# The lower part of every third weight chunk in the first layer's mixers made by an adding DMA instead of VectorE, with rings one deeper

## The chip, the cores and the metric

The kernel runs on one core of one Trainium2 chip. The time is that of the device, in microseconds (us), as the median of several runs. In the profile PE is TensorE's matmul, PEld its weight load, DVE is VectorE, ACT ScalarE, POOL GpSimd, and SP the engine that issues the loads.

## The reference

Two layers of a block on x of 256 × 1024 numbers in f32. Each layer normalizes x, multiplies it by one wide matrix, and feeds the pieces to three mixers: attention with low-rank projections (8 heads), gated linear attention (GLA, 4 heads) and a diagonal state-space scan (S5). Their outputs, each through a projection of its own, are merged by sigmoid gates and projected once more; a feed-forward part with a squared relu follows.

```python
for l in range(2):
    h = rms_norm(x, norm1_g[l])
    z = h @ w_in[l]
    (cq, ckv, kpe, gq, gk, gv, glr, gr, su, gates) = split_in(z)
    o_a = mla_mixer(cq, ckv, kpe, ...)        # attention
    o_b = gla_mixer(gq, gk, gv, glr, gr, ...) # gated linear attention
    o_c = s5_mixer(su, ...)                   # scan over a complex diagonal state
    g = sigmoid(gates + gate_b[l]).reshape(B, L, 3, D)
    merged = g[:, :, 0] * (o_a @ w_br_mla[l]) + g[:, :, 1] * (o_b @ w_br_gla[l]) + g[:, :, 2] * (o_c @ w_br_s5[l])
    x = x + merged @ w_out[l]
    h2 = rms_norm(x, norm2_g[l])
    x = x + square(relu(h2 @ w_ff1[l])) @ w_ff2[l]
```

## The kernel before

All weights of both layers stand in one tensor in memory, `wst`, as chunks of 128 × 1024 f32 numbers (512 KB; three chunks per layer are 128 × 768). The kernel goes through them once, in one stream of 276 chunks, 138 per layer: 73 for the mixers, gates and projections, then 64 for the feed-forward part. A chunk's place in the stream is called k here. The order is written out by hand in the table STEPS: each word is a step (su, qk, gv, gr for projections of x; s0 to s3 and y for the scan; h and p for the scores and the values of a head; g for gates; b for the branch projections; o for the output), a number behind "~" shifts the priority of its instructions. A scheduler turns the priorities into one fixed order of instructions on each engine, when the kernel is built.

A matmul is done in three passes on numbers cut into an upper and a lower part (`mm3`, L184 to L186): upper by upper, upper by lower, lower by upper. So each weight chunk passes through these stations:

- `fetch` (L144) issues the load of the chunk from SP's queue into a ring of three `raw` tiles.
- `prep` (L153) makes the two parts: ScalarE casts raw into hi (L164), rounded to the upper part, and VectorE subtracts, lo = raw − hi (L165).
- PE reads hi and lo. They live in two rings of NHI = 4 tiles each, and when the stream stands at chunk k, the chunks up to k + AHEAD, with AHEAD = 3, are prepared. A cast waits until PE is done with the chunk that held its place in the ring.

Beside the chunks, ScalarE and VectorE do the work of the mixers. Early in the first layer the function around L406 to L418 makes the S5 matrices: VectorE computes complex products in z, ScalarE spreads them into bbar (L418), PE transposes bbar into Btp (L453). At the same time the GLA gate runs through ScalarE: ab (L947, L948), the scan cs on VectorE (L951), the exponentials ep, en, dec (L956 to L960), with a load of the activation table ahead of some. In the softmax, ScalarE computes ppt (L875, exponentials, and L879, their scaling), PE transposes it into PTp. POOL only clears tiles and copies the scan's coefficients into R (L606).

Of the kernel before, what the change touches and what calls it, by code (L numbers as in the profile page):

```python
# [8 lines left out]
F32 = mybir.dt.float32  # L9
# [4 lines left out]
AF = mybir.ActivationFunctionType  # L14
ALU = mybir.AluOpType
# [40 lines left out]
CIDX = {c: i for i, c in enumerate(CHUNKS)}  # L56
# [30 lines left out]
class Kern:  # L87
# [67 lines left out]
    def prep(self, k):  # L155
        nc = self.nc
        l, c = self.stream[k]
        n = CCOLS.get(c[0], CW)
        self.prefetch(k + 1)
        raw = self.raws[k]  # L160
        hi = self.ring.tile([128, CW], F32R, tag="hi", name="hi", bufs=self.NHI)
        lo = self.ring.tile([128, CW], F32R, tag="lo", name="lo", bufs=self.NHI)
        for h in self.halves(k, n):
            nc.scalar.copy(hi[:, h], raw[:, h])  # L164
            nc.vector.tensor_tensor(out=lo[:, h], in0=raw[:, h], in1=hi[:, h].bitcast(F32), op=ALU.subtract)  # L165
        return hi, lo

    def w(self, l, c):
        assert self.stream[self.pos] == (l, c), (self.stream[self.pos], l, c)
        self.prepare(self.pos + 1 + self.AHEAD)  # L170
        t = self.prepped[self.pos]
        self.prepped[self.pos] = None
        self.pos += 1
        return t
# [989 lines left out]
    NPS = {"g": 2, "ps": 2, "acc": 4}  # L1164
    NSM = {"gv": 2, "v": 2, "gt": 2, "tmp": 3}
    NRAW = 3
    NHI = 4
    AHEAD = 3


    STEPS = [
# [194 lines left out]
    Kern(ctx, tc, aps).run()  # L1366


# [13 lines left out]
```

## Time and profile before

| what | us |
| --- | --- |
| median of 3 runs | 882.55 |
| lowest and highest | 882.38, 883.68 |
| profiled execution | 882.19 |
| its span, first to last instruction | 880.4 |
| PE busy | 861.7 |
| VectorE busy | 694.5 |
| ScalarE busy | 522.0 |
| POOL busy | 25.4 |

The mean granted clock of TensorE is 0.998 of full speed. Busy times are those of the profiled execution; matmuls overlap, so a group's sum of durations is larger than the time that it takes from the span. The stretches of the first layer are, roughly: start to 20 us; projections, GLA and the S5 matrices to 105; scan, attention and the first gates to 200; gates, branch and output projections to 265; the feed-forward part to 450. The second layer follows in the same manner.

### The profile page before, as it was taken

To read this page: it belongs to the slowest core of one execution; us is meant where nothing else is said; L and a number is where in the kernel's file an instruction comes from. 1 tells how busy PE (TensorE), PEld (TensorE's weight loads), DVE (VectorE), ACT (ScalarE), POOL (GpSimd) and SP (SyncE) were. 2 spreads that over 40 slices of the span, in tenths; PEclk is the share of its full clock that TensorE was granted. 3 is DMA by queue.
4 is the path that set the end of the run, shared out by engine and by line. 5 is a ranking of instruction groups with operands and counts; after the bars stand their busy time and mean duration, and the time that the engine had idled before them with its cause. 6 is when DMAs were issued, how large, how long until landed. Compare 5 with 4: busy or idle time off the path is not lost.

```text
span 880.4 us, 15290 instructions
## 1 busy us (share of the span) xinstructions
PE 861.7 (98%) x5900; PEld 771.2 (88%) x5900; DVE 694.5 (79%) x1339; ACT 522.0 (59%) x818; POOL 25.4 (3%) x35
## 2 busy tenths in 40 slices
PE   7999999999999999999999999999999999999998
PEld 6889988899988888888888989898999888888886
DVE  7999999987767986996677887899877776666664
ACT  6877887654456575664457647874554654444442
POOL 2000001010000000000000000002000000000000
PEclk9999999999999999999999999999999999999999
DMA  7534434245564565566545544244555555555562
GB/s 265 188 118 143 154 121 145 72 153 177 189 210 153 186 212 168 182 189 203 190 146 168 191 146 150 97 144 135 178 166 170 191 181 192 189 189 188 192 190 92
DMA packets 42264, 147.73 MB, mean 168 GB/s; under 512 B 4688, under 2 KB 5328, under 8 KB 42192
## 3 DMA queue, kind: packets, MB, share of 16 engines
q1 hardware_dynamic: 42192, 146.76, 51.6%
q8 instruction: 46, 0.75, 0.3%
q14 instruction: 26, 0.21, 0.1%
HBM read 145.70 MB, written 1.05 MB: 167 GB/s over the span
## 4 chain that ended last, share of the span: by engine, by line
PE 84%; DVE 10%; ACT 3%; issue 2%; DMA 1%; SPq 0%; DVEq 0%
PE fp L206 14%; PE fp L210 7%; PE fo L184 7%; PE fo L186 7%; PE fo L185 7%; PE gp L184 3%; DVE lo L165 3%; PE gp L185 3%; PE gp L186 3%; PE brp L184 2%; PE brp L186 2%; PE brp L185 2%; PE wo L186 2%; PE wo L184 2%; PE wo L185 2%
## 5 line engine op out<-in xcount | busy, mean ns | idle before, releaser
L165 DVE TENSOR_TENSOR lo<-raw,hi 128x1024 fp32r<-128x1024 f32 (+2 forms) x276 | 333.0, 1208 | 118.6 <-ACT hi L164 117.5
L164 ACT CAST hi<-raw 128x1024 fp32r<-128x1024 f32 (+2 forms) x276 | 286.1, 1038 | 234.0 <-PE fo L186 52.9
L206 PE MATMUL fp<-h,hi 128*128 128x512 f32 x512 | 180.5, 398 | 0.0
L210 PE MATMUL fp<-h,lo 128*128 128x256 f32 x512 | 133.5, 281 | 0.0
L184 PE MATMUL gp<-h,hi 128*128 128x256 f32 x384 | 109.9, 292 | 1.0 <-ACT ppt L875 0.8
L206 PEld LDWEIGHTS fp<-h,hi 128*128 128x128 f32 x512 | 93.9, 188 | 18.1
L186 PE MATMUL gp<-h,lo 128*128 128x256 f32 x384 | 107.8, 286 | 0.0
L185 PE MATMUL gp<-h,hi 128*128 128x256 f32 x384 | 107.4, 285 | 0.0
L210 PEld LDWEIGHTS fp<-h,lo 128*128 128x128 f32 x512 | 96.8, 189 | 5.5
L184 PE MATMUL fo<-hi,r 128*128 128x512 f32 x256 | 100.1, 391 | 0.0
L186 PE MATMUL fo<-hi,r 128*128 128x512 f32 x256 | 99.7, 390 | 0.0
L185 PE MATMUL fo<-lo,r 128*128 128x512 f32 x256 | 99.7, 389 | 0.0
L184 PEld LDWEIGHTS gp<-h,hi 128*128 128x128 f32 x384 | 72.7, 192 | 2.9 <-ACT ppt L875 1.0
L185 PEld LDWEIGHTS gp<-h,hi 128*128 128x128 f32 x384 | 72.6, 191 | 1.0 <-issue 0.5
L186 PEld LDWEIGHTS gp<-h,lo 128*128 128x128 f32 x384 | 72.7, 192 | 0.1
L185 PEld LDWEIGHTS fo<-lo,r 128*128 128x128 f32 x256 | 48.1, 188 | 10.1
L186 PEld LDWEIGHTS fo<-hi,r 128*128 128x128 f32 x256 | 48.1, 188 | 10.2
L184 PEld LDWEIGHTS fo<-hi,r 128*128 128x128 f32 x256 | 48.1, 188 | 8.8
L1133 ACT COPY fa<-fp 128x256 f32<-128x256 f32 x64 | 23.4, 367 | 29.3 <-PE fp L206 29.1
L1134 DVE TENSOR_TENSOR fa<-fa,fp 128x256 f32<-128x256 f32 x64 | 26.2, 416 | 13.7 <-ACT fa L1133 13.7
L1071 ACT ACTIVATE gt<-gt,hgateb 128x256 f32<-128x256 f32 x48 | 21.9, 501 | 9.0 <-DVE gt L1068 8.8
L256 ACT CAST r<-fa 128x512 fp32r<-128x512 f32 x32 | 19.9, 622 | 9.7 <-DVE fa L1135 9.5
(396 smaller groups left out, 1768.0 us busy)
## 6 DMA issues: line engine op xcount, KB each, us to landing
raw<-wst SPq DMA_DIRECT2D x266, 512.0 KB, 3.6
raw<-wst SPq DMA_DIRECT2D x6, 384.0 KB, 3.0
x<-xin SPq DMA_DIRECT2D x4, 256.0 KB, 4.6
raw<-wst SPq DMA_DIRECT2D x4, 256.0 KB, 5.6
bc_raw<-bcin SPq DMA_DIRECT2D x4, 256.0 KB, 3.8
out_dram<-x SPq DMA_DIRECT2D x4, 256.0 KB, 2.0
par<-parin SPq DMA_DIRECT2D x2, 205.0 KB, 5.8
masks<-consts SPq DMA_DIRECT2D x1, 128.0 KB, 3.8
```

The costliest lines, as they stand in the source:

```text
L164: nc.scalar.copy(hi[:, h], raw[:, h])
L165: nc.vector.tensor_tensor(out=lo[:, h], in0=raw[:, h], in1=hi[:, h].bitcast(F32), op=ALU.subtract)
L184: mm(out, lhsT=lt[0], rhs=rt[0], start=start, stop=False)
L185: mm(out, lhsT=lt[0], rhs=rt[1], start=False, stop=False)
L186: mm(out, lhsT=lt[1], rhs=rt[0], start=False, stop=stop)
L206: up = lambda: mm(flat, lhsT=w[0][:, c], rhs=self.h2[:, k].rearrange("p i t -> p (i t)"), start=k == 0, stop=k == KD - 1)
L210: mm(out[:, 0, :], lhsT=w[1][:, c], rhs=self.h[k][0], start=False, stop=False)
L256: nc.scalar.copy(hi, src)
L1071: nc.scalar.activation(g[:, m, :], g[:, m, :], AF.Tanh, scale=0.5, bias=self.small[l]["gateb"][:, c:c + 1])
L1133: nc.scalar.copy(a[:, m], p[:, 1, :])
L1134: self.mark = v.tensor_tensor(out=a[:, m], in0=a[:, m], in1=p[:, 0, :], op=ALU.add)
```

## The change

For 23 chunks, every third from k = 9 to k = 75, the lower part is no longer made by VectorE. ScalarE casts raw into hi as before, then writes −hi into lo, and POOL issues a DMA that adds the chunk from memory onto lo. The load of raw stays, so these chunks are transferred twice. One of the 23 is 128 × 768, the rest are 128 × 1024. Both rings have five tiles, and chunks are prepared four ahead. The last hunk sets the memory for descriptors of such transfers. Lines of the changed kernel below `prep` stand eight higher.

```diff
         hi = self.ring.tile([128, CW], F32R, tag="hi", name="hi", bufs=self.NHI)
         lo = self.ring.tile([128, CW], F32R, tag="lo", name="lo", bufs=self.NHI)
+        if self.by_dma(k):
+            nc.scalar.copy(hi[:, 0:n], raw[:, 0:n])
+            nc.scalar.activation(lo[:, 0:n], hi[:, 0:n].bitcast(F32), AF.Copy, scale=-1.0)
+            nc.gpsimd.dma_start(lo[:, 0:n], self.wst[l, CIDX[c], :, 0:n], accum_op=ALU.add)
+            return hi, lo
         for h in self.halves(k, n):
             nc.scalar.copy(hi[:, h], raw[:, h])
             nc.vector.tensor_tensor(out=lo[:, h], in0=raw[:, h], in1=hi[:, h].bitcast(F32), op=ALU.subtract)
         return hi, lo
+
+    def by_dma(self, k):
+        return 8 < k < 76 and k % 3 == 0
...
-    NHI = 4
-    AHEAD = 3
+    NHI = 5
+    AHEAD = 4
...
+BACC_KW = {"dynamic_dma_scratch_size": 4096}
...
-    nc = bacc.Bacc("TRN2", target_bir_lowering=False, num_devices=1)
+    nc = bacc.Bacc("TRN2", target_bir_lowering=False, num_devices=1, **BACC_KW)
```

The instructions move on ScalarE and POOL. First ScalarE ahead of the S5 matrices bbar and the Btp transposes, between the gate's logarithm (ab) and its exponentials (ep, en, dec); z with a number is VectorE's product, cmat the other S5 matrix. Before:

```order
L948 ACT_TABLE_LOAD
L948 ACTIVATE ab<-ab,half 128x512
L164 CAST hi<-raw 128x1024
L956 ACT_TABLE_LOAD
L956 ACTIVATE ep<-cs 128x512
L957 ACTIVATE en<-cs 128x512
L960 ACTIVATE dec<-cs 128x8
L164 CAST hi<-raw 128x1024
L418 ACTIVATE bbar<-z_476 64x16x16 x4
L164 CAST hi<-raw 128x1024
L418 ACTIVATE bbar<-z_477 64x16x16 x4
L418 ACTIVATE cmat<-z_478 64x16x16 x2
```

And after the change:

```order
L956 ACT_TABLE_LOAD
L956 ACTIVATE ab<-ab,half 128x512
L164 CAST hi<-raw 128x1024
L165 ACTIVATE lo<-hi 128x1024
L169 CAST hi<-raw 128x1024
L426 ACTIVATE bbar<-z_482 64x16x16 x4
L169 CAST hi<-raw 128x1024
L426 ACTIVATE bbar<-z_483 64x16x16 x4
L426 ACTIVATE cmat<-z_484 64x16x16 x2
L964 ACT_TABLE_LOAD
L964 ACTIVATE ep<-cs 128x512
```

The table load and the exponentials moved from ahead of bbar to behind it; the scaled copy lo (L165) came in, and one cast went further up.

Next ScalarE in the gates of the first layer, after the gate's first tanh pieces; tg belongs to the S5 output gate, oc is a branch's input. Before:

```order
L259 ACTIVATE oc<-tg 128x512
L164 CAST hi<-raw 128x1024 x2
L675 ACTIVATE tg<-glup,hbglu 128x256 x2
L164 CAST hi<-raw 128x1024
L259 ACTIVATE oc<-tg 128x512
L1071 ACTIVATE gt<-gt,hgateb 128x256 x2
```

And after:

```order
L169 CAST hi<-raw 128x1024 x2
L683 ACTIVATE tg<-glup,hbglu 128x256 x2
L164 CAST hi<-raw 128x1024
L267 ACTIVATE oc<-tg 128x512
L165 ACTIVATE lo<-hi 128x1024
L169 CAST hi<-raw 128x1024 x2
L683 ACTIVATE tg<-glup,hbglu 128x256 x2
```

Behind the cast of each chunk of the new kind (L164) stands a scaled copy (L165), sometimes with a piece of other work in between; the other casts (L169) are as before.

Last POOL in the first layer, where s5r is the scan's coefficient and K, cmat and bbar are tiles cleared for the second layer. Before:

```order
L606 COPY R<-s5r_355 128x512
L607 MEMSET R 128x4
L465 MEMSET K_4192 128x512
L424 MEMSET cmat 128x2048
L423 MEMSET bbar 128x2048
```

And after:

```order
L166 DMA lo<-wst 128x1024 x2
L614 COPY R<-s5r_361 128x512
L615 MEMSET R 128x4
L166 DMA lo<-wst 128x1024
L473 MEMSET K_4221 128x512
L166 DMA lo<-wst 128x1024
L432 MEMSET cmat 128x2048
L166 DMA lo<-wst 128x1024 x2
L431 MEMSET bbar 128x2048
L166 DMA lo<-wst 128x1024 x7
```

Ten transfers stand ahead of these rows and thirteen in them; they are queued in order between the copies into R, which wait for VectorE, and the memsets, which wait for PE.

## Rows read from the trace of the kernel before

**Rows 1.** The page's first part: busy time of each engine, its share of the span and its instructions.

```profile
PE 861.7 (98%) x5900; PEld 771.2 (88%) x5900; DVE 694.5 (79%) x1339; ACT 522.0 (59%) x818; POOL 25.4 (3%) x35
```

**Rows 2.** The page's fourth part: the chain that ended last, its share by engine.

```profile
PE 84%; DVE 10%; ACT 3%; issue 2%; DMA 1%; SPq 0%; DVEq 0%
```

**Rows 3.** The view by stretches of the span. Columns: the stretch (us), its length, busy us (and instructions) of PE, weight load, VectorE, ScalarE and POOL, the granted TensorE clock, the busy share of the DMA engines, GB/s.

```profile
20.00:105.00 85.00, 82.81 (x640) 74.57 (x639) 79.03 (x250) 64.98 (x100) 0.72 (x2) 0.98 0.46 150
105.00:200.00 95.00, 90.41 (x827) 83.54 (x826) 89.79 (x186) 66.50 (x129) 8.63 (x8) 1.00 0.40 127
200.00:265.00 65.00, 65.00 (x473) 61.60 (x472) 46.13 (x58) 33.34 (x44) 1.81 (x1) 1.00 0.60 193
...
450.00:700.00 250.00, 247.79 (x1980) 231.58 (x1979) 208.77 (x398) 152.70 (x248) 7.42 (x8) 1.00 0.48 155
```

**Rows 4.** What PE waited for, over the whole span. Columns: engine, tile and line that waited, what released it; us in total, times, longest.

```profile
PE Btp L453 <- issue: 2.2, 1, 2.2
PE PTp L887 <- ACT ppt L879: 1.7, 3, 1.1
...
PE gp L184 <- ACT ppt L875: 0.8, 1, 0.8
```

**Rows 5.** Stretches of one and of three microseconds around the Btp transposes, columns as in rows 3.

```profile
44.00:45.00 1.00, 0.00 (x0) 0.00 (x0) 1.00 (x4) 0.98 (x3) 0.00 (x0) 1.00 0.11 41
46.00:47.00 1.00, 1.00 (x9) 1.00 (x10) 1.00 (x3) 0.98 (x3) 0.00 (x0) 0.88 0.00 0
47.00:50.00 3.00, 3.00 (x13) 2.71 (x13) 2.54 (x5) 2.93 (x7) 0.00 (x0) 0.50 0.00 0
50.00:51.00 1.00, 1.00 (x9) 0.83 (x8) 1.00 (x2) 0.73 (x2) 0.00 (x0) 0.92 0.00 0
```

**Rows 6.** Stretches of one microsecond in the softmax, where PE also has a gap.

```profile
132.00:133.00 1.00, 0.41 (x4) 0.42 (x4) 1.00 (x4) 0.87 (x3) 0.00 (x0) 1.00 0.79 107
133.00:134.00 1.00, 1.00 (x11) 1.00 (x10) 1.00 (x3) 1.00 (x5) 0.00 (x0) 1.00 0.77 311
```

**Rows 7.** The timeline of ScalarE ahead of the Btp transposes, and as the last row that of PE. Columns: start, duration, engine, line, operation, tile and shape, count.

```profile
38.42 1.28 ACT L956 ACT_TABLE_LOAD   x1
...
41.28 1.04 ACT L164 CAST hi<-raw 128x1024 fp32r<-128x1024 f32 x1
42.32 1.70 ACT L418 ACTIVATE bbar<-z 64x256 f32<-64x256 f32 x4
44.05 1.04 ACT L164 CAST hi<-raw 128x1024 fp32r<-128x1024 f32 x1
45.00 1.71 ACT L418 ACTIVATE bbar<-z 64x256 f32<-64x256 f32 x4
...
45.93 1.17 PE L453 MATMUL Btp<-con,bbar 128*128 128x128 f32 x8 [2.16 <-issue]
```

**Rows 8.** The timeline of VectorE in the same stretch (37.5 to 44 us).

```profile
37.50 0.69 DVE L949 TENSOR_TENSOR mn<-mn,ab 128x512 f32<-128x512 f32 x1 [0.64 <-ACT ab L948]
...
38.86 1.22 DVE L951 TENSOR_TENSOR_SCAN cs<-cmask,mn 128x512 f32<-128x512 f32 x1
...
40.06 1.22 DVE L165 TENSOR_TENSOR lo<-raw,hi 128x1024 fp32r<-128x1024 f32 x1
...
43.55 0.42 DVE L408 TENSOR_TENSOR z<-z,z 128x256 f32<-128x256 f32 x1
```

**Rows 9.** What the softmax activations on ScalarE waited for between 105 and 200 us, columns as in rows 4.

```profile
ACT ppt L875 <- DVE anb L873: 4.4, 4, 3.0
...
ACT ppt L879 <- DVE arec L877: 2.7, 2, 1.5
```

**Rows 10.** The groups of VectorE and of ScalarE by shape, between 8 and 265 us: the subtraction, the cast, and the one activation of a chunk's shape. Columns: line, engine, operation, tile, shape, count | busy us, mean ns | idle time before, releaser.

```profile
L165 DVE TENSOR_TENSOR lo<-raw,hi 128x1024 fp32r<-128x1024 f32 x69 | 84.0, 1219 | 16.1 <-ACT hi L164 15.8
...
L164 ACT CAST hi<-raw 128x1024 fp32r<-128x1024 f32 x70 | 73.0, 1047 | 52.6 <-PE gp L185 11.9 <-PE brp L185 10.5 <-PE glup L185 6.7
...
L658 ACT ACTIVATE u<-u 128x1024 f32<-128x1024 f32 x1 | 1.1, 1062 | 0.0
```

**Rows 11.** The view by stretches for the 12 us before the table load that leads to the gate's logarithm.

```profile
20.43:32.56 12.13, 12.13 (x77) 10.31 (x76) 11.51 (x55) 8.04 (x12) 0.00 (x0) 1.00 0.65 210
```

**Rows 12.** The casts of the weight chunks between 105 and 200 us, as a group.

```profile
L164 ACT CAST hi<-raw 128x1024 fp32r<-128x1024 f32 x22 | 22.9, 1048 | 10.4 <-PE gp L185 5.1 <-DMA raw<-wst 3.3 <-PE brp L185 1.8
```

**Rows 13.** The page's sixth part: the loads of the weight chunks. Columns: tile, queue, operation, count, KB each, median us from issue to landing.

```profile
raw<-wst SPq DMA_DIRECT2D x266, 512.0 KB, 3.6
```

**Rows 14.** The timeline of POOL: its copy into R, at two of its eight places.

```profile
33.40 0.61 POOL L606 COPY R<-s5r 128x512 f32<-128x512 f32 x1 [20.15 <-DVE s5r L349]
...
603.90 4.40 POOL L606 COPY R<-s5r 128x512 f32<-128x512 f32 x1 [18.13 <-DVE rot L620]
```

**Rows 15.** The timeline of ScalarE in the gates: two casts of weight chunks.

```profile
215.43 1.05 ACT L164 CAST hi<-raw 128x1024 fp32r<-128x1024 f32 x1 [0.50 <-PE brp L185]
218.31 1.05 ACT L164 CAST hi<-raw 128x1024 fp32r<-128x1024 f32 x1 [1.83 <-PE gp L185]
```

**Rows 16.** The timeline of PE in the gates: the third matmul of a group (the one that reads a lower part) in three chunks.

```profile
220.99 0.28 PE L186 MATMUL brp<-ob,lo 128*128 128x256 f32 x1
...
221.35 0.28 PE L186 MATMUL gp<-h,lo 128*128 128x256 f32 x1
...
222.39 0.28 PE L186 MATMUL brp<-oc,lo 128*128 128x256 f32 x1
```

## The prediction

> **What bounds the kernel now.** I read the page's engine line first: TensorE is busy for 861.7 of 880.4 us, VectorE for 694.5, ScalarE for 522.0 [rows 1]. The chain that ended last says the same, 84% PE and 10% DVE [rows 2]. A change that leaves the matmuls as they are can therefore win only from the 18.7 us in which PE is idle, from the time it runs at the lower clock, and it can lose wherever PE has to wait anew. So the next view is the table of stretches, to see where that idle time lies [rows 3]: 85.00 − 82.81 = 2.19 us in 20 to 105 us, 95.00 − 90.41 = 4.59 us in 105 to 200, nothing in 200 to 265, 2.21 us in 450 to 700, which is the second layer and is not touched. The 23 chunks of the change are used between 39 and 275 us, so at most 2.19 + 4.59 us of idle time are within its reach.
>
> The waits of PE give these idle times names [rows 4]. The 2.2 us at 20 to 105 are one gap, ahead of the Btp transposes, put down to "issue". The view by short stretches shows it, PE at 0.00 in 44 to 45, and what follows it: the granted clock is 0.88 in 46 to 47, 0.50 in the three microseconds to 50 and 0.92 in 50 to 51, that is the 1.2 GHz level for a little over three microseconds instead of 2.4 [rows 5]. Their shortfall is 0.12 + 3 × 0.50 + 0.08 = 1.7 us of work at full clock. The other gaps are shorter and cost no clock: PE works 0.41 of the window 132 to 133, and the grant stays 1.00 there and after [rows 6].
>
> What does Btp wait for? The ScalarE timeline answers better than the releaser: the second group of bbar writes begins at 45.00, and 0.93 us later, with two of its four instructions done, Btp starts at 45.93 [rows 7]. VectorE had the numbers for it at 43.55 + 0.42 = 43.97 [rows 8]. So ScalarE's queue is late there by about a microsecond, VectorE next.
>
> In 105 to 200 us VectorE is busy for 89.79 of 95 us [rows 3], and the softmax activations wait for it, 4.4 and 2.7 us in all [rows 9]; PE's waits for those activations (PTp 1.7, gp 0.8) follow [rows 4].
>
> **The change, part by part.** Each of the 23 chunks takes one subtraction of 1.22 us off VectorE and puts on ScalarE one scaled copy, which the trace does not show in this form; the nearest row is an activation of the same shape, 1.06 us [rows 10]. Its cast stays.
>
> First term, the Btp gap. By the order of ScalarE after the change, the table load of 38.42 and the three exponentials, which lasted until the cast at 41.28, move behind bbar: 41.28 − 38.42 = 2.86 us leave the path. What comes ahead of bbar by the change is one cast and two scaled copies: 1.05 + 2 × 1.06 = 3.2 us. That would be no gain if ScalarE were full, but in the 12.13 us before 32.56 it is busy for only 8.04 [rows 11], and by the order one of the copies and two of the casts now stand there. On VectorE two subtractions and the scan, 3 × 1.22 us [rows 8], leave the stretch ahead of bbar and three trigonometric pieces come in, at 0.69 each by the nearest row of their shape [rows 8], so its numbers come 3.7 − 2.1 = 1.6 us earlier. I take Btp at 44.7 instead of 45.93: 1.2 us of gap gone. The remaining gap of 0.9 us is as short as those that cost no clock [rows 6], so the 1.7 us go too. Together −2.9 us. The bounds: nothing, if the two copies delay ScalarE by as much as the table load did, and 2.2 + 1.7 = −3.9, if the gap closes.
>
> Second term, 105 to 200 us. 22 chunks are cast there [rows 12], and of these about 8 are of the new kind (the 30th to the 51st of the stream): VectorE has 8 × 1.22 = 9.8 us less of 89.8. The softmax waits should shrink, and the idle time of PE with them, at best by all 4.6 us. But on ScalarE 8 × 1.06 = 8.5 us come into the same queue as the softmax activations, which have to stand behind a copy now and then. The two are of one size, and I take 0 for both, with ends of −4.6 and +8.5.
>
> Third term, when the lower part is there. The chain of one such chunk is cast 1.05, copy 1.06, the POOL engine's issue, and the landing. The trace has no POOL transfer. A plain load of the same 512 KB takes 3.6 us from issue to landing [rows 13]; an adding one has to fetch the source, read the old value and write the sum, and if each of the three cost a whole load it would take 3 × 3.6 = 10.8, an estimate. For the issue the nearest row is POOL's copy into R, 0.61 us alone and 4.40 at the worst [rows 14]; I take 0.61 and 3.6, so the chain is 6.3 us. The room: in 200 to 265 us the casts go out every 2.88 us, each when PE frees a slot [rows 15], and with rings of five a chunk is cast four turns before it is read: 4 × 2.88 = 11.5 us. Two of the nine DMA chunks of that stretch (the 57th and 69th of the stream) are read by PE one turn early, as with the gp chunk that begins inside the turns of brp [rows 16]: 3 × 2.88 = 8.6 us for these. Earlier, in 105 to 200 us, a turn is longer, 95 / 22 = 4.3 us [rows 12], and the room 17. So 6.3 us fits with 2.3 to spare: cost 0. What hides it is the deeper ring alone; without it the room would be 2.88 us less, and two chunks would be late by 0.6 us each. At the upper ends the price is heavy, since PE has no idle time there to absorb it: at a landing of 10.8 the chain is 13.5, late by 4.9 us on two chunks and 2.0 on seven, +23.8 us.
>
> The DMA engines: their share in 200 to 265 is 0.60 [rows 3]. One chunk in three is now transferred a second time; if that costs as much as a load, the share becomes 0.60 × 4/3 = 0.80, at two times the cost 1.00, at three 1.20, 13 us over. I take the first.
>
> A rule of the Trainium skill speaks against that choice: the page "DMA: Bandwidth & Descriptors", section "Rules for kernel authors", says that an accumulating DMA reads its destination and writes it later. No run here shows it yet. If this made the transfer twice as long as the plain load, 7.2 us, the chain would be 9.9 and two chunks would be late by 1.3 us each, +2.6, and the forecast about 881.9 instead of 879.3.
>
> POOL's queue is in order, and the transfers stand between its copies into R, which wait for VectorE, and its memsets, which wait for PE. In 105 to 200 us the room of 17 us less the chain of 6.3 leaves such a transfer 10 us to stand behind one of them, so I cost this at nothing. SP's loads go one chunk further ahead; nothing waits for that.
>
> The sum against the profiled execution's 882.2 us: −2.9 + 0 + 0 gives 879.3. The median of the runs shown, 882.55, is 0.3 above that execution, which I leave inside the range. What cannot be told from no change is ±0.2%, 1.8 us: 880.8 to 884.3.
>
> **The rivals.** (a) Slower: the adding transfer lands too late in the gates and the output projection, 200 to 275 us. For it: PE there has no slack at all and the DMA share is already 0.60 [rows 3]. Against it: a plain load is far within the room. It decides from where the lateness eats the 2.9 us: 2 × (chain − 8.6) = 2.9 at a chain of 10.05, a landing of 7.3 us. At 9 us the chain is 11.7, the price 2 × 3.1 + 7 × 0.2 = 7.6, and the time 882.2 − 2.9 + 7.6 = 887. (b) No change: ScalarE gains nothing ahead of bbar, since the added 3.2 us stand against the removed 2.86, the clock falls as before, and the rest is covered: 882.2. For it: PE is 98% busy. Against it: ScalarE's idle time before 32.6 us. (c) Slower by ScalarE: each of the 8 copies in 105 to 200 stands ahead of a softmax activation: 882.2 − 2.9 + 8.5 = 888. Against it: ScalarE is busy for only 66.5 of these 95 us. (d) POOL is held up by VectorE at each issue, as its copy into R was at 603.90 [rows 14]: the issue takes 4.40 instead of 0.61, the chain is 10.1, two chunks are late by 1.5 us each, 882.2 − 2.9 + 3.0 = 882.3. The Trainium skill has this as a rule ("SBUF — State Buffer", section "SBUF: two separate sides"): VectorE in certain modes locks GpSimd out of a shared port, and its descriptors stay unwritten. That slow copy agrees with a lock; that it falls on descriptors no run here shows.
>
> **How the numbers follow.** The forecast with its near neighbours (the first term between −1.8 and −3.9, some of the second won) has 0.48; (b) 0.14, (d) 0.06, which both end within 1.8 us; (a) 0.22, (c) 0.10. So faster 0.48, the same 0.20, slower 0.32. The likeliest case's own range is 874 (all of both terms, 882.2 − 3.9 − 4.6 = 873.7) to 880.8. The whole range goes down to 873 and up to 891, beyond (a) and (c) at their prices; landings above 9.5 us lie outside.
>
> **What would show it.** In the profile after: PE's gap ahead of Btp under 1 us and no stretch at 0.50 from 46 to 50; PE idle in 105 to 200 at 4.6 us or less; PE still full in 200 to 265 with no wait for lo; the lo transfers from POOL landing in under 7 us with a DMA share near 0.80. Waits of PE for the DMA of lo, a share near 1.0, or casts late for raw would make the forecast wrong on the slow side, softmax waits on ScalarE likewise; VectorE's relief turning into PE time in 105 to 200 would make it too high.

## The result, and the profile after

The changed kernel is slower: 894.68 us as the median of four runs (891.67 to 895.77), against 882.46 for the kernel before in the same session. The ratio is 1.013, with a 95% interval of 1.0103 to 1.0157. The forecast was 879.3 and its range ended at 891. The profile shown here is of the fastest of the four executions, 891.67 us with a span of 889.9; it has a mean granted clock of 0.998, the other three have 0.994 to 0.996.

The page's engine line and the chain that ended last, against [rows 1] and [rows 2]:

```profile
PE 864.3 (97%) x5900; PEld 770.7 (87%) x5900; DVE 672.4 (76%) x1316; ACT 542.4 (61%) x841; POOL 44.6 (5%) x58
...
PE 79%; DVE 9%; ACT 6%; DMA 4%; issue 2%; SPq 0%; DVEq 0%; ACTq 0%; POOLq 0%
```

VectorE lost 22.1 us of work and ScalarE got 20.4 more, as intended, and PE's share fell. PE's idle time is 889.9 − 864.3 = 25.6 us instead of 18.7. The chain has new shares for ScalarE (6% instead of 3%) and for transfers (4% instead of 1%).

The stretches, columns as in [rows 3]. The last is moved by the delay, so that it holds the same work; the first holds less than before, 593 matmuls instead of 640, and that of the gates ends 7 us later:

```profile
20.00:105.00 85.00, 78.63 (x593) 68.84 (x591) 73.48 (x246) 68.72 (x106) 7.38 (x9) 0.98 0.67 188
105.00:200.00 95.00, 91.26 (x831) 84.17 (x830) 78.31 (x173) 72.85 (x136) 13.38 (x15) 1.00 0.61 163
200.00:272.00 72.00, 69.12 (x505) 65.22 (x504) 41.56 (x52) 43.25 (x54) 8.72 (x9) 1.00 0.87 244
459.00:709.00 250.00, 247.50 (x1976) 230.99 (x1974) 208.10 (x398) 152.30 (x247) 7.41 (x8) 1.00 0.48 155
```

PE is idle for 6.37 us in 20 to 105 (2.19 before), 3.74 in 105 to 200 (4.59) and 2.88 in the gates (0). Over the work that 105 to 200 held before (110.5 to 205.4 here) it is idle for 4.0. The second layer is as it was, 2.50 against 2.21. The DMA share in the gates rose from 0.60 to 0.87.

What PE waited for, columns as in [rows 4]:

```profile
PE PTp L895 <- ACT ppt L887: 2.7, 3, 1.3
PE Btp L461 <- issue: 2.5, 1, 2.5
...
PE wo L193 <- DMA lo<-wst: 1.6, 1, 1.6
PE kgp L192 <- DVE gqk L918: 1.6, 1, 1.6
PE stp L720 <- ACT sqc L714: 1.6, 1, 1.6
...
PE gp L194 <- DMA lo<-wst: 1.0, 1, 1.0
```

The gap ahead of Btp did not close, it is 2.5 us. New are a wait for gqk on VectorE, one for sqc on ScalarE, and two for the adding transfers, 1.0 and 1.6 us.

Where time is lost can be read as places, from the timelines of PE: the start of the first matmul into four tiles, and the span. The rows of the experiments belong to the next section; e12_again is the changed kernel once more. In the last three kernels ten matmuls of brp stand ahead of glup that stand behind it elsewhere, 0.12 us each or 1.2 us of work, so their way from glup to fp compares with each other and not with the rest.

| kernel | Btp | gp | glup | fp | span |
| --- | --- | --- | --- | --- | --- |
| before | 45.93 | 94.17 | 198.86 | 270.39 | 880.4 |
| after | 47.94 | 99.62 | 204.30 | 279.26 | 889.9 |
| e12_again | 46.42 | 99.72 | 205.08 | 278.08 | 888.7 |
| e1_ring | 48.06 | 95.89 | 204.86 | 276.37 | 886.6 |
| e6_early | 47.64 | 99.31 | 203.99 | 275.88 | 886.8 |
| e7_gates | 48.56 | 97.02 | 206.06 | 279.29 | 890.2 |
| e13_late_ring | 47.23 | 94.76 | 200.63 | 271.82 | 882.0 |
| e14_late_gates | 47.16 | 94.68 | 200.37 | 275.63 | 893.5 |
| e16_late_five | 47.35 | 94.86 | 200.51 | 272.01 | 882.4 |

The changed kernel is behind by 2.0 us at Btp, 5.5 at the first gate chunk, still 5.4 at glup, and 8.9 at the start of the feed-forward part; then little more is added. So two stretches lose, the first 95 us and the last gates with the output projection, and the stretch of softmax and scan, where VectorE was full, neither wins nor loses.

### The profile page after: what moved, and what is told of

It reads as the page before. It is cut to its first block, busy times and chain, and to the rows that moved or that the text cites. A ratio compares the mean times of both kernels' runs of the same rounds, so it can differ in the third digit from the quotient of the medians.

```text
span 889.9 us, 15311 instructions
## 1 busy us (share of the span) xinstructions
PE 864.3 (97%) x5900; PEld 770.7 (87%) x5900; DVE 672.4 (76%) x1316; ACT 542.4 (61%) x841; POOL 44.6 (5%) x58
## 3 DMA queue, kind: packets, MB, share of 16 engines
HBM read 157.62 MB, written 1.05 MB: 178 GB/s over the span
## 4 chain that ended last, share of the span: by engine, by line
PE 79%; DVE 9%; ACT 6%; DMA 4%; issue 2%; SPq 0%; DVEq 0%; ACTq 0%; POOLq 0%
PE fp L214 13%; PE fp L218 7%; PE fo L194 7%; PE fo L192 7%; PE fo L193 7%; PE gp L192 3%; PE gp L194 3%; PE gp L193 3%; DVE lo L170 2%; PE brp L192 2%; PE brp L194 2%; PE brp L193 2%; DMA raw<-wst 2%; PE wo L193 2%; PE wo L194 2%
## 5 line engine op out<-in xcount | busy, mean ns | idle before, releaser
L170 DVE TENSOR_TENSOR lo<-raw,hi 128x1024 fp32r<-128x1024 f32 (+2 forms) x253 | 305.3, 1208 | 125.2 <-ACT hi L169 124.4
L169 ACT CAST hi<-raw 128x1024 fp32r<-128x1024 f32 (+2 forms) x253 | 262.3, 1038 | 211.1 <-PE fo L194 50.5
L164 ACT CAST hi<-raw 128x1024 fp32r<-128x1024 f32 (+1 forms) x23 | 23.9, 1037 | 13.7 <-PE gp L193 5.3
L166 POOL DMA_DIRECT2D lo<-wst x23 | 20.2, 876 | 218.9 <-ACT lo L165 130.8
```

The source lines that it names most:

```text
L164: nc.scalar.copy(hi[:, 0:n], raw[:, 0:n])
L166: nc.gpsimd.dma_start(lo[:, 0:n], self.wst[l, CIDX[c], :, 0:n], accum_op=ALU.add)
```

## The experiments

**The rings alone.** Theory A was that the deeper rings cost by themselves; theory B, that all the cost is the transfers'. e1_ring is the changed kernel without any adding transfer:

```diff
-        return 8 < k < 76 and k % 3 == 0
+        return False
```

> Rings of five and preparation four ahead, but all lower parts by VectorE as before. Theory A (the deeper rings cost by themselves: casts stand one chunk earlier in ScalarE's queue, which is in order, and wait there for PE or for a load while other work is behind them; that cost the changed kernel some 4 to 5 us in the first 105 us): 886 to 888 us, PE idle in 20 to 105 us 5 to 6.5 us instead of 2.2, the gap ahead of Btp as long as before. Theory B (the cost is all from the adding transfers and what they do to the loads): 882 to 883 us, PE idle in 20 to 105 us about 2.2.

Measured: 888.71 us, ratio 1.0068 (1.0053 to 1.0083). The deeper rings alone cost 5.8 us, nearly half of the changed kernel's 12.2, so B falls. By the places they cost it in two pieces: 1.7 us up to the first gp and 4.3 more between gp and glup. ScalarE's timeline shows the first (start, duration, engine, line, operation; in brackets the idle time before and what ended it):

```profile
30.05 1.05 ACT L169 CAST hi<-raw 128x1024 fp32r<-128x1024 f32 x1 [2.37 <-PE kgp L194]
...
36.14 1.28 ACT L955 ACT_TABLE_LOAD   x1
...
47.13 1.70 ACT L426 ACTIVATE bbar<-z 64x256 f32<-64x256 f32 x4
```

The cast at 30.05 had waited for 2.37 us until PE was done with kgp and a place in the ring came free. It stands ahead of the S5 work in ScalarE's queue, and the table load for the gate's tanh comes at 36.14; in the kernel before it came at 32.56, the end of [rows 11]. The second group of bbar follows at 47.13 instead of 45.00 [rows 7].

The second piece is one gap in the softmax, with the lower clock behind it: a wait of PE, and two stretches.

```profile
PE gp L192 <- DVE arec L885: 2.6, 1, 2.6
...
174.00:175.00 1.00, 0.00 (x0) 0.00 (x0) 1.00 (x3) 1.00 (x2) 0.00 (x0) 1.00 0.00 0
...
177.00:178.00 1.00, 1.00 (x7) 1.00 (x6) 1.00 (x2) 0.21 (x1) 0.00 (x0) 0.50 0.79 262
```

PE waits for arec on VectorE, which is busy without a pause. PE has no such wait in the changed kernel, so not all of the 5.8 us can be a part of its loss. Why the deeper ring brings it about, by VectorE's load or by another order of the instructions, is not shown.

e5_nhi5 has the deeper rings with the old look-ahead:

```diff
-        return 8 < k < 76 and k % 3 == 0
+        return False
...
-    AHEAD = 4
+    AHEAD = 3
```

> Rings of five tiles, but preparation three ahead as before, no adding transfer. If the loss of e1_ring (5.8 us) is that casts and subtractions stand one chunk earlier in the queues of ScalarE and VectorE: 882 to 884 us, kgp and Btp at their old times within 0.5 us. If the deeper ring itself (another order from the scheduler) is at fault: 887 to 890.

Measured: 886.21 us, 1.0034 (1.0021 to 1.0047), between the two answers. About half of the 5.8 us comes with the fifth tile alone and half with the look-ahead; the expectation had put all of it to one of them. In its profile PE does not wait for arec, and it is 2.0 us behind at fp (272.35 against 270.39), so the second half is the gap in the softmax.

e13_late_ring keeps rings of four and a look-ahead of three up to k = 47 and adds the fifth tile from there on:

```diff
-        hi = self.ring.tile([128, CW], F32R, tag="hi", name="hi", bufs=self.NHI)
+        fifth = k >= 48 and k % 5 == 0
+        hi = self.ring.tile([128, CW], F32R, tag="hx" if fifth else "hi", name="hi", bufs=1 if fifth else self.NHI)
...
-        self.prepare(self.pos + 1 + self.AHEAD)
+        self.prepare(self.pos + 1 + self.AHEAD + (self.pos >= 47))
```

> Rings of four and preparation three ahead up to k = 47, and from k = 48 on a fifth tile in both rings and preparation four ahead; all lower parts by VectorE. If the loss of e1_ring comes from the first 200 us (casts in front of the S5 matrices, the gates and the softmax): 882 to 883.5, as before. If a deeper ring costs wherever it is: 886 to 889.

Measured: 883.95 us, 1.0011 (1.0001 to 1.002), half a microsecond above the lower answer and far from the upper. A deeper ring is nearly free from the gates on. Its cost lies in the first 190 us, where ScalarE and VectorE have other work behind the casts.

**The transfers without the rings.** e2_ring4 has all 23 transfers with rings of four and a look-ahead of three:

```diff
-    NHI = 5
-    AHEAD = 4
+    NHI = 4
+    AHEAD = 3
```

> The adding transfers for the same 23 chunks, but rings of four and preparation three ahead as before. Theory A: the early loss is gone, but each of the nine transfers in the gates has 2.9 us less room: the chain measured in the changed kernel is 8 to 10 us, the room 5.7 to 8.6, so 5 to 25 us of waits of PE for the lower part there; 890 to 905 us. Theory B: no less than the changed kernel's 894.7 and the loss of the first 105 us stays.

Measured: 919.74 us, 1.0434 (1.0405 to 1.0462), above theory A's range, and theory A's "the early loss is gone" did not come true: the first gp starts at 105.18 us, 11.0 behind the kernel before. PE's waits for lo are 10.8 us in six pieces at gp, 4.7 in two at wo and 4.0 at fp, that for sqc is 3.6, and the mean granted clock fell to 0.988. So these transfers need the deeper rings. One thing does differ early: without the deeper rings the table load for the tanh comes at 33.67 us and the second group of bbar at 44.61, 0.4 earlier than before and not 2.0 later; the gap ahead of Btp is 0.4 us. But PE then waits 2.1 us for Bt, which ScalarE copies out of Btp, and the clock falls behind that wait.

**Which transfers cost.** e6_early, e3_mid and e7_gates are the changed kernel with the transfers of one stretch each (the bounds of k in `by_dma`: 8 to 30, 29 to 52, 52 to 76); e4_mid_ring4 and e11_four have rings of four and a look-ahead of three, with k between 29 and 52 and between 38 and 50. The edit of e11_four:

```diff
-        return 8 < k < 76 and k % 3 == 0
+        return 38 < k < 50 and k % 3 == 0
...
-    NHI = 5
-    AHEAD = 4
+    NHI = 4
+    AHEAD = 3
```

> Rings of five, preparation four ahead, adding transfers only for the seven chunks k = 9 to 27, read up to 105 us. By the places in the changed kernel's trace (PE behind the kernel before by 5.5 us at 95 us, e1_ring by 1.7) these transfers cost 3.8 us: 892 to 893. The rival, that the early part costs nothing but by the rings: 888 to 889.

> Rings of five, and adding transfers only for the eight chunks from k = 30 to k = 51, which are read between 105 and 200 us. Theory A: as e1_ring, less up to 1 us that VectorE's relief gives between 105 and 200 us: 885 to 888. Theory B: 881 to 883.

> Rings of five, preparation four ahead, adding transfers only for the eight chunks k = 54 to 75, read in the gates and the output projection. If late lower parts there cost what the changed kernel's trace shows (PE waits of 1.0 and 1.6 us for the transfer, 3.4 us by the places between 199 and 270 us): 891 to 893, with the waits of PE for lo at k = 57 and 69. If they are covered, as forecast: 888.7 as e1_ring, within 1 us.

> As e3_mid, but with rings of four and preparation three ahead. Theory A: nothing is lost early, the transfers have more than 10 us of room: 880 to 883 us. Theory B: the same as e3_mid within 1 us.

> Rings of four and preparation three ahead as before, adding transfers only for the four chunks k = 39 to 48, where a slot is free longest before its lower part is read and VectorE is fullest. If a transfer in time is free and VectorE's relief is worth something: 881 to 882.5. If the copies on ScalarE or the traffic cost even there: 884 to 886.

Measured: e6_early 888.93 us (1.0071, 1.0056 to 1.0086), the same as e1_ring, so the seven early transfers add nothing in sum. But by the places it is 3.4 us behind e1_ring at the first gp: by a wait of 1.5 us for sqc that the changed kernel has too, and by the low clock behind the Btp gap, which e1_ring's profile lacks. Right ahead of that sqc ScalarE has a table load of 1.28 us and an activation of 0.63 that do not stand there in the kernel before. e1_ring loses as much later, in the softmax, and e6_early does not. The two kernels are equal by two different losses, and that of e6_early is the one that the changed kernel shows (5.1 us behind at gp, against its 5.5).

e3_mid took 886.73 us (1.0042, 1.0027 to 1.0057), 2.0 under e1_ring; its PE does not wait for arec, and waits 2.2 us in two pieces for lo. e7_gates took 893.01 (1.0124, 1.01 to 1.0147), 4.3 above e1_ring, at the upper end of its first answer. Its waits for lo are smaller than in the changed kernel, 0.3 us at gp and 0.7 at wo, and by the places its way from glup to fp is only 1.7 us longer than that of e1_ring; 1.1 us came before any of its transfers, with the lower clock behind the Btp gap, which e1_ring's profile lacks. So not all of the 4.3 is theirs.

e4_mid_ring4 took 885.26 us (1.0027, 1.0018 to 1.0036), which theory A had not expected. Its profile gives the reason, the chunk k = 33, on PE's timeline:

```profile
131.88 0.39 PE L194 MATMUL gp<-h,lo 128*128 128x256 f32 x1 [1.90 <-DMA lo<-wst]
```

The lower part landed 1.90 us late, and right behind it the granted clock fell, in the view by stretches:

```profile
133.00:137.00 4.00, 4.00 (x23) 4.00 (x23) 4.00 (x9) 4.00 (x10) 0.00 (x0) 0.57 0.44 151
```

That is 4 × 0.43 = 1.7 us more. e11_four leaves out that chunk and the others with less room: 882.13 (0.9993, 0.9984 to 1.0002). There the stretch of VectorE's relief looks like this:

```profile
105.00:200.00 95.00, 91.51 (x833) 84.43 (x832) 87.49 (x188) 70.25 (x133) 9.52 (x12) 1.00 0.52 149
```

PE idles 3.49 us instead of 4.59 [rows 3], and the time cannot be told from the kernel before. So a transfer in time, without the deeper ring, costs nothing and brings at most 0.16%.

**The prices by themselves.** e8_traffic and e9_neg are e1_ring, with VectorE making every lower part, and one cost added for the same 23 chunks. In e8_traffic an adding transfer goes into a tile that nobody reads:

```diff
+        if self.by_dma(k):
+            d = self.dummy
+            nc.scalar.copy(d[:, 0:1], hi[:, 0:1])
+            nc.gpsimd.dma_start(d[:, 0:n], self.wst[l, CIDX[c], :, 0:n], accum_op=ALU.add)
```

In e10_plain the last line has no `accum_op`. In e9_neg the scaled copy alone goes into such a tile:

```diff
+        if self.by_dma(k):
+            d = self.ring.tile([128, CW], F32R, tag="dummy", name="dummy", bufs=1)
+            nc.scalar.activation(d[:, 0:n], hi[:, 0:n].bitcast(F32), AF.Copy, scale=-1.0)
```

> As e1_ring, all lower parts by VectorE; beside them the same 23 adding transfers go into a tile that nobody reads, each after a one-column copy on ScalarE (0.2 us), so traffic alone is added. If the transfers hold up the loads of raw enough to matter: 2 to 7 us above e1_ring's 888.7. If only ScalarE's copies and late lower parts count: 888 to 890.

> As e8_traffic, with the same order of instructions on every engine, but the 23 extra transfers are plain copies into the tile that nobody reads instead of adding ones. If an adding transfer costs nearly twice a plain one (in the changed kernel 5.8 us of a transfer engine's time per MB against 3.0 for the loads): landing 3.5 to 5 us instead of 7.3, 3 to 6 us less than e8_traffic's 899.2. If the extra cost is that of GpSimd's queue: landing 6.5 to 7.5 and 898 to 900.

> As e1_ring, all lower parts by VectorE; for the 23 chunks ScalarE also writes the scaled copy, into a tile that nobody reads, and there is no transfer. If ScalarE's copies delay what is behind them (the squares sqc, the softmax): 3 to 6 us above e1_ring's 888.7. If not: 888 to 890.

Measured: e9_neg 891.85 us (1.0098, 1.0083 to 1.0113), 3.1 above e1_ring. The copies count, and the gap ahead of Btp is where it shows first, in the waits of PE:

```profile
PE Btp L459 <- issue: 4.2, 1, 4.2
```

e8_traffic took 899.21 us (1.0176, 1.0159 to 1.0193), 10.5 above e1_ring, more than expected. Its queues and issues on the page (packets, MB, share of 16 engines; then count, KB each, median us from issue to landing):

```profile
q1 hardware_dynamic: 42192, 146.76, 51.3%
q0 software_dynamic: 3312, 11.93, 7.8%
...
raw<-wst SPq DMA_DIRECT2D x266, 512.0 KB, 4.2
dummy<-wst POOLq DMA_DIRECT2D x22, 512.0 KB, 7.3
```

And those of e10_plain, 893.11 us (1.0119, 1.0105 to 1.0133), 6.1 less than e8_traffic:

```profile
q1 hardware_dynamic: 42192, 146.76, 49.9%
q0 software_dynamic: 3312, 11.93, 4.6%
...
raw<-wst SPq DMA_DIRECT2D x266, 512.0 KB, 3.6
dummy<-wst POOLq DMA_DIRECT2D x22, 512.0 KB, 4.8
```

The same bytes as an adding transfer take 7.8% instead of 4.6% of the 16 engines, 1.7 times as much, and land in 7.3 instead of 4.8 us; the loads beside them land in 4.2 instead of 3.6. ScalarE's casts waited for loads for 28.0 us in the first 280 us of e8_traffic, against 9.0 in e1_ring. The price of 10.5 us is too high for the changed kernel, since the one-column copy on ScalarE itself waited for the transfer before it, 5.8 us in four pieces.

**Lateness or traffic in the gates.** e14_late_gates, e15_late_six and e16_late_five are e13_late_ring with `by_dma` for k = 54 to 75 in threes, then without 57 and 69, then also without 75:

```diff
-        return False
+        return k in (54, 60, 63, 66, 72)
```

> As e13_late_ring, with adding transfers for the eight chunks k = 54 to 75. If the loss in the gates is the late lower part of the 57th and the 69th and the full DMA engines there: 3 to 5 us above e13_late_ring, with PE waits for lo. If it came from the early part by way of the lower clock: as e13_late_ring within 1 us.

> As e14_late_gates without the 57th and the 69th, the two that PE reads one turn early. If only their lateness counts: as e13_late_ring within 1 us, no PE wait for lo. If the traffic counts by itself: 2 us or more above e13_late_ring.

> As e15_late_six without the 75th, whose scaled copy stood behind the norm on ScalarE and whose lower part PE awaited for 5.1 us in the feed-forward part; the transfers for k = 54, 60, 63, 66 and 72 remain. If a transfer costs only where its lower part is late: as e13_late_ring within 1 us (883 to 885), no PE wait for lo. If the traffic or the copies cost by themselves in the gates: 887 or more.

Measured: e14_late_gates 895.38 us (1.0147, 1.0121 to 1.0172), e15_late_six 892.0 (1.0098, 1.0079 to 1.0117), e16_late_five 885.42 (1.0032, 1.0019 to 1.0045). The first lost far more than expected, because of the chunk k = 75. The other two late ones are there as well, and by the places its way from glup to fp takes 75.26 us instead of 71.19 in e13_late_ring. Waits of PE in e14_late_gates:

```profile
PE fp L219 <- DMA lo<-wst: 4.0, 1, 4.0
...
PE wo L194 <- DMA lo<-wst: 1.8, 1, 1.8
PE gp L195 <- DMA lo<-wst: 1.7, 1, 1.7
```

The scaled copy of k = 75 stood behind the norm on ScalarE, its lower part was 4.0 us late, and the clock fell behind that gap:

```profile
282.00:285.00 3.00, 0.00 (x0) 0.00 (x0) 0.00 (x0) 0.00 (x0) 0.00 (x0) 0.92 0.82 164
286.00:291.00 5.00, 5.00 (x17) 4.27 (x16) 0.22 (x1) 1.30 (x2) 0.00 (x0) 0.50 0.00 0
```

e15_late_six is without the waits at gp and wo, but has that of 5.1 us at fp, so its verdict on traffic is lost. e16_late_five has no wait for lo; in its profile the way from glup to fp takes 71.50 us, as in e13_late_ring (71.19), at a DMA share of 0.79 in 200 to 272. Its median is 1.5 us above e13_late_ring, and 2.2 when each is taken against the kernel before of its own session (2.9 and 0.7): between the two answers of the expectation. The profile, the fastest execution, does not show where. So most of what is lost here is lateness; whether the traffic or the copies cost the other one or two microseconds stays open.

**The same kernel again.** e12_again is the changed kernel, unaltered.

> The changed kernel once more, for a second profile. If its four times differ by stretches at the lower clock behind the gaps of PE: idle time within 1 us of the first profile's 25.6 us, and the difference in span is that of the stretches at the lower clock, at 1.5 to 2 us each.

Measured: 890.44 us, below the lowest of the first four, span 888.7. Both parts of the expectation were wrong. The idle time is 22.4 us, not within 1 us of 25.6: the wait for gqk and that for lo at gp are absent, and that for lo at wo is 0.6 us. And the span is 1.2 us shorter, although there is one low stretch more, behind the wait for sqc:

```profile
88.00:89.00 1.00, 0.00 (x0) 0.00 (x0) 0.15 (x1) 0.99 (x4) 0.00 (x0) 1.00 0.37 29
...
92.00:94.00 2.00, 2.00 (x6) 1.54 (x6) 1.16 (x12) 1.53 (x3) 0.86 (x1) 0.50 0.31 124
```

In the first profile PE was idle for 1.6 us at the same place, and 91 to 95 us had the clock at 1.00. What both profiles have is the gap ahead of Btp (2.5 and 2.6 us) with the low stretch behind it, the wait for sqc, and 5.5 us of delay at the first gp.

## Why the prediction was wrong

**First term, the Btp gap (−2.9 us predicted): the wrong step.** The order came as read: on ScalarE bbar stands ahead of the exponentials. But the text took ScalarE's idle time before 32.56 us as room ("in the 12.13 us before 32.56 it is busy for only 8.04"), and that time was waiting. Two pieces of it, on ScalarE's timeline of the kernel before:

```profile
22.98 1.05 ACT L164 CAST hi<-raw 128x1024 fp32r<-128x1024 f32 x1 [1.50 <-PE gqkp L186]
...
27.86 0.22 ACT L368 ACTIVATE s5s<-s5th 128x16 f32<-128x16 f32 x1 [0.77 <-DVE s5th L356]
```

ScalarE's timeline of the changed kernel:

```profile
24.67 1.05 ACT L169 CAST hi<-raw 128x1024 fp32r<-128x1024 f32 x1 [2.74 <-DMA raw<-wst]
...
30.67 1.05 ACT L164 CAST hi<-raw 128x1024 fp32r<-128x1024 f32 x1 [2.47 <-PE kgp L194]
...
37.51 1.28 ACT L955 ACT_TABLE_LOAD   x1
...
44.34 1.69 ACT L426 ACTIVATE bbar<-z 64x256 f32<-64x256 f32 x4
...
47.01 1.70 ACT L426 ACTIVATE bbar<-z 64x256 f32<-64x256 f32 x4
```

The cast at 24.67 waited for 2.74 us for its load, the one at 30.67 for 2.47 us for a place in the ring, and both hold what is behind them. The table load came at 37.51 instead of 32.56, and moving 2.86 us of work behind bbar could not make up for 4.95. (Of the loads of raw the forecast had said "nothing waits for that".) Btp started at 47.94, not at the forecast 44.7, behind a gap of 2.5 us, and the low clock came as before:

```profile
49.00:50.00 1.00, 1.00 (x6) 0.81 (x5) 0.89 (x2) 0.97 (x3) 0.00 (x0) 0.64 0.15 29
50.00:52.00 2.00, 2.00 (x11) 2.00 (x11) 0.46 (x1) 1.98 (x4) 0.00 (x0) 0.50 0.02 4
52.00:53.00 1.00, 1.00 (x8) 1.00 (x7) 0.32 (x2) 0.99 (x3) 0.00 (x0) 0.65 0.00 0
```

That is 0.36 + 2 × 0.50 + 0.35 = 1.7 us of shortfall, as in [rows 5]. How late Btp starts differs between executions (46.42 in e12_again, with the table load at 35.98), but the gap stays in both. Rival (b), "ScalarE gains nothing ahead of bbar", was the better reading: in e2_ring4, with the transfers and without the deeper rings, the second group of bbar comes only 0.4 us earlier than before, not 1.2. With the deeper rings it comes 2.0 us later in the changed kernel (0.5 in e12_again) and 2.1 in e1_ring.

**A term that was missing: the rings.** The forecast priced the fifth tile and the longer look-ahead at nothing and counted them only as cover. e1_ring shows 5.8 us for them, of which the changed kernel's profile has the early piece.

**Second term, 105 to 200 us (0 predicted): right.** From the first gp to glup the lag went from 5.45 to 5.44 us. VectorE went from 89.79 to 78.31 us busy, and PE's idle time from 4.59 to 4.0 over the same work. That the two effects would be of one size was a guess, and no run separates them. Rival (c), eight copies each in front of a softmax activation, did not happen at its price of 8.5.

**Third term, the lower part in time (0 predicted): wrong, by the landing and by the room.** The queues and issues of the changed kernel:

```profile
q1 hardware_dynamic: 42192, 146.76, 50.2%
q0 software_dynamic: 3312, 11.93, 7.8%
...
raw<-wst SPq DMA_DIRECT2D x266, 512.0 KB, 3.6
lo<-wst POOLq DMA_DIRECT2D x22, 512.0 KB, 6.5
```

An adding transfer lands in 6.5 us, not the 3.6 taken from [rows 13]. That time is counted from the start of the issue, so the issue (0.86 us, not 0.61) is in it, and the prediction's formula counts it twice. With the measured sizes the chain is 1.05 + 1.06 + 6.5 = 8.6, just as long as the room of the two short chunks: no more than on the brink. PE waits at just those two, k = 57 (gp) and k = 69 (wo), 1.0 and 1.6 us, but what makes them late is ScalarE's queue. The first, on ScalarE, POOL and PE:

```profile
218.11 1.05 ACT L164 CAST hi<-raw 128x1024 fp32r<-128x1024 f32 x1 [1.09 <-PE gp L193]
...
220.39 1.04 ACT L165 ACTIVATE lo<-hi 128x1024 fp32r<-128x1024 f32 x1
...
221.73 0.86 POOL L166 DMA_DIRECT2D lo<-wst  x1 [4.54 <-ACT lo L165]
...
228.09 0.39 PE L194 MATMUL gp<-h,lo 128*128 128x256 f32 x1 [1.02 <-DMA lo<-wst]
```

The copy starts 1.2 us after the cast has ended, since other work of ScalarE stands between them, and the whole chain takes 228.09 − 218.11 = 10.0 us. The second:

```profile
254.34 1.70 ACT L426 ACTIVATE cmat<-bc_raw 64x256 f32<-64x256 f32 x4 [2.13 <-DMA bc_raw<-bcin]
256.06 1.05 ACT L164 CAST hi<-raw 128x1024 fp32r<-128x1024 f32 x1
...
264.31 0.50 PE L193 MATMUL wo<-lo,mh 128*128 128x512 f32 x1 [1.60 <-DMA lo<-wst]
```

Here the chain is 264.31 − 256.06 = 8.2 us, within the forecast's room. But the cast did not go out when PE freed its place: four copies for the second layer stood ahead of it and had waited 2.13 us for a load, and 264.31 − 1.60 − 256.06 = 6.65 us of room were left. It is the wrong step of the first term once more.

The rule of the Trainium skill (page "DMA: Bandwidth & Descriptors", section "Rules for kernel authors") that an accumulating DMA reads its destination was the better guide to the landing: the estimate from it was 7.2 us. That the 2.6 us which followed from it are also the sum of the two waits is luck; in e12_again the same two are 0 and 0.6 us.

**The rivals.** (a) had the right sign and place, but not the whole: from glup to fp the changed kernel lost 3.4 us, 2.6 of them in the two waits for lo. (d), POOL held up by VectorE, did not happen: the 23 issues took 0.86 to 1.01 us each, so the lock that the Trainium skill describes ("SBUF — State Buffer", section "SBUF: two separate sides") does not show at them. Whether VectorE was in one of the modes meant there no run tells.

**The sum.** Rings 5.8 (e1_ring); on top of them early transfers 0.2, mid ones −2.0, those in the gates 4.3: together 8.3 us, against 12.2 measured. But the pieces do not simply add up, since each of these kernels loses at places of its own. In the profile of the changed kernel, the fastest of the four, the 9.5 us of span are 5.5 up to the first gp, where e6_early (rings and early transfers) has 5.1; nothing up to glup; 3.4 to fp, with the two waits for lo; and 0.6 behind it. The other 3 us between that execution and the median are not separated. The five executions lie between 890.44 and 895.77 us, and of the first four the slower ones have the lower mean clock, so part of it is likely more stretches at the lower clock, as e12_again shows one; that is argued, not shown for these runs. That e12_again ends inside the forecast's range is luck: the gap ahead of Btp and the low stretch behind it, which made up the forecast's gain, are still there.

## What to carry to other kernels

Idle time of an engine whose queue is in order is not room: ask what each idle piece waits for before counting on it, because one more instruction of the prefetch ahead of it waits too, and takes all that is behind it along. Deepen a ring where the queue has little else behind the prefetch (here from the gates on, 0.7 us), not where it has (5.8 us with the whole stream). Taking work off a busy engine that is not the one that bounds the time brings little (at most 0.16% in e11_four), and what replaces it has to be in time at every single chunk: one late chunk can also cost the clock behind it, as in e4_mid_ring4.

## What was not expected of the hardware

The lower clock behind a gap of PE is not certain. PE was idle for 2.16 us ahead of Btp in the kernel before and the clock fell; it was idle for about 2.6 us there in e1_ring, and the clock stayed:

```profile
46.00:48.00 2.00, 0.00 (x0) 0.00 (x0) 2.00 (x7) 1.94 (x5) 0.00 (x0) 1.00 0.00 0
48.00:52.00 4.00, 3.24 (x26) 3.06 (x27) 3.51 (x6) 3.90 (x9) 0.00 (x0) 1.00 0.00 0
```

A gap of 1.90 us in e4_mid_ring4 was followed by 1.7 us of shortfall, and the wait for sqc in the changed kernel, 1.6 us in the first profile and 1.5 in e12_again, was followed by a low stretch only the second time. So one profile shows one outcome. Kernels with more such gaps may well spread more (4.1 us among the four executions of the changed kernel, 1.4 us among the four of the kernel before); but fifteen of the kernel before spread by 2.6, so this is not shown.

POOL took the same 0.86 us to issue nearly every adding transfer, with VectorE busy for 78.31 of 95 us, while its own copies into R took from 0.61 to 4.40 us [rows 14].
